# A dense trunk kernel: inside a chunk of weights the rounded-format products come first, then each f16 correction together

## The chip, the cores and the metric

The kernel runs on one core of one Trainium2 chip. Its time is the device time of one execution in microseconds; three executions took 3231.93, 3232.30 and 3233.21 us, median 3232.3 us. The trace comes from one more, profiled execution of the same program.

Five engines work side by side and are joined by semaphores: PE (TensorE, matrix products; its weight loads are listed as PEld), ACT (ScalarE), DVE (VectorE), POOL (GpSimd) and SP (SyncE, which here only issues DMAs). Each takes its own instructions in the order in which they stand in its queue.

## The reference

512 tokens of width 1024 pass through two layers. Everything is float32. Cut to what matters here:

```python
for layer in range(2):
    proj = h @ w_in[layer]                       # 1024 -> 11 776 columns, split into 14 parts
    y_a = (silu(rg) * rms_norm(retention(rq, rk, rv))) @ ret_w_out[layer]
    y_b = (silu(hg) * rms_norm(hgrn2_scan(hq, log_f, h_k, h_v)) * g) @ hgrn_w_out[layer]
    y_c = swa_with_sinks(sq, sk, sv) @ swa_w_out[layer]
    merged = sigmoid(ga) * y_a + sigmoid(gb) * y_b + sigmoid(gc) * y_c
    h = layer_norm(ALPHA * h + merged @ w_o[layer])
    ff = swiglu(h) if layer == 0 else moe_swiglu(h)   # dense 2816, then top 2 of 8 experts of 3584
    h = layer_norm(ALPHA * h + ff)
```

The dense products are all the `@` of this loop but the experts: `w_in`, the three branch projections, `w_o`, and the first layer's feed-forward block.

## The kernel before

**Three products for one.** A float32 product is made of three that PE takes at a higher pace. A weight chunk arrives as float32 (`raw`) and is split in three: `whi`, the value rounded to PE's fp32r format; `wlo`, what the rounding left, as f16; and a third part, the value itself as f16, which stands in the second half of the tile `wlo`. The activations are split alike: `hThi` (fp32r), `hTlo` (f16 rest) and `hT` (f16 value; `br...`, `fin...` and `hid...` are the same three for other activations). A dense product is then whi*hThi + (rest of w)*(f16 x) + (f16 w)*(rest of x), summed in one PSUM bank. I call the first the rounded product and the other two the corrections. Three such matmuls for one slice of 128 input rows are a triple.

**How the work is tiled.** Input rows come in 8 slices k of 128 (22 for the second product of the feed-forward block). A chunk of weights is 128x1024 numbers: in `proj_f` it is one block of 128 output columns over all 8 slices, the weights stand in the array and 512 tokens stream past (8 triples). In `proj_t` the activations stand in the array (128 tokens j out of 4) and 512 output columns stream; there a chunk holds 2 slices of k, and four PSUM banks, one for each j, fill together. `proj_t` holds the last four chunks of a product at once and goes through them j by j, 8 triples for one j; the 22 slices of the feed-forward block begin with seven chunks that are taken one at a time (4 j x 2 slices, 8 triples each). `proj_f_halves` works like `proj_f` on 256 tokens at a time. So nearly all dense work comes in groups of 8 triples.

**What sets the order.** PE's order is the order of the code (a hand-made schedule; small tasks of the mixers are slipped in by `soon`, `tick` and `need`). ACT, DVE and POOL are ordered by the framework's scheduler, so that their order may move when PE's does. `Stream` prepares weights: DMA into `raw` (L209), ACT writes `whi` (L226), DVE `wlo` (L227), ACT the f16 value (L234); there are five sets of `whi`/`wlo`, and `proj_t` holds four of them. After a layer norm the activations are turned by PE (L307), and `split` writes their three parts: ACT L355 (`hThi`), ACT L356 (`hT`), DVE L357 (`hTlo`); `need(j)` puts those turns of token block j into PE's queue. Every matmul of the program is recorded at L302. The experts of the second layer have code of their own (`accumulate`, `by_row`), with all rounded products of a chunk ahead of its corrections; `gu` is their PSUM tile.

Of the kernel before, what the change touches and what calls it, by code (L numbers as in the profile page):

```python
# [21 lines left out]
P = 128  # L22
D = 1024
S = 512
NJ = S // P
KD = D // P
# [164 lines left out]
class Stream:  # L191
# [58 lines left out]
    def done(self):  # L250
        self.held = 0
        self.fill()
# [5 lines left out]
def body(tc, A, out, dbg=None):  # L258
# [50 lines left out]
    T = PE  # L309
# [12 lines left out]
    def tick(budget=4.0):  # L322
        end = PE.clock + budget
        while PE.clock < end:
            due = [t for t in later if t[0] <= PE.clock]
            if not due:
                return

            task = max(due, key=lambda t: getattr(t[1], "prio", 0))
            later.remove(task)  # L330
            task[1](*task[2])
# [24 lines left out]
        SC.activation(x16, src, AF.Copy, scale=1.0 / (DS * LS))  # L356
        V.scalar_tensor_tensor(lo, hi.bitcast(F32), -DS * LS, src, op0=OP.mult, op1=OP.add)  # L357

    def mm3(ps, w, x, first, last):
        T.matmul(ps, w[0], x[0], start=first, stop=False)  # L360
        T.matmul(ps, w[1], x[2], start=False, stop=False)
        T.matmul(ps, w[2], x[1], start=False, stop=last)

    hbuf = []
    turns = {}
# [42 lines left out]
    def need(*js):  # L408

        for j in js:  # L410
            if j in turns:
                turns.pop(j)()
# [7 lines left out]
    def new_hT():  # L420
        hi = hpool.tile([P, KD, S], FR, name="hThi")
        lo = hpool.tile([P, KD, S], F16, name="hTlo")
        x16 = hpool.tile([P, KD, S], F16, name="hT16")
        return hi, lo, x16
# [6 lines left out]
    def proj_f(hT, kn=KD):  # L431
        need(*range(NJ))
        w = stream.next()
        ps = psA.tile([P, S], F32, name="acc")
        for k in range(kn):
            sl = slice(k * P, (k + 1) * P)
            mm3(ps, [t[:, sl] for t in w], [t[:, k] for t in hT], k == 0, k == kn - 1)
        tick()
        return ps


    def proj_f_halves(hT, n):
        ws = stream.take(n)
        pss = []
        for i in range(n):
            ps = psA.tile([P, S], F32, name="acc")
            pss.append(ps)
        need(0, 1)
        for th in range(2):
            tk = slice(256 * th, 256 * th + 256)  # L450
            for i, (ps, w) in enumerate(zip(pss, ws)):
                if th == 0 and i >= n - 2:
                    need(i - n + 4)
                for k in range(KD):
                    sl = slice(k * P, (k + 1) * P)
                    mm3(ps[:, tk], [t[:, sl] for t in w], [t[:, k, tk] for t in hT], k == 0, k == KD - 1)
        stream.done()
        return pss


    def proj_t(xT, kn, per, n, done=None):
        pss = []
        for j in range(NJ):
            ps = psA.tile([P, n], F32, name="acc")
            pss.append(ps)

        def tile_(j, k, w, q):
            tj = slice(j * P, (j + 1) * P)
            sl = slice(q * n, (q + 1) * n)
            T.matmul(pss[j], xT[0][:, k, tj], w[0][:, sl], start=(k == 0), stop=False)  # L470
            T.matmul(pss[j], xT[2][:, k, tj], w[1][:, sl], start=False, stop=False)
            T.matmul(pss[j], xT[1][:, k, tj], w[2][:, sl], start=False, stop=(k == kn - 1))

        nch = kn // per
        last = min(4, nch)
        for c in range(nch - last):
            need(*range(NJ))
            w = stream.next()
            for j in range(NJ):
                for q in range(per):  # L480
                    tile_(j, c * per + q, w, q)
            tick()
        ws = stream.take(last)
        for j in range(NJ):
            need(j)
            for i, w in enumerate(ws):
                if i == last - 1:
                    need(j + 1)
                for q in range(per):
                    tile_(j, (nch - last + i) * per + q, w, q)  # L490
            if j == NJ - 1:
                stream.done()
            if done is not None:
                done(j, pss[j])
            tick()
        return pss

    def out_ln(pool, xT, kn, per, g_ap, b_ap, nxt, after=None):
        gb = pool.tile([P, D], F32, name="ln_g", bufs=1)
        SC.dma_start(gb, rows(g_ap))  # L500
        bb = pool.tile([P, D], F32, name="ln_b", bufs=1)
        SC.dma_start(bb, rows(b_ap))
        V.tensor_scalar(bb, bb, LS, None, op0=OP.mult)
        old = hbuf[0]
        rs = []
        for j in range(NJ):
            r = pool.tile([P, D], F32, name="ln_r", bufs=4)
            SC.dma_start(r, old[j * P:(j + 1) * P])
            rs.append(r)
        new_hbuf(nxt)  # L510
        hT = new_hT()

        def done(j, ps):
            sl = slice(512 * half, 512 * half + 512)
            V.scalar_tensor_tensor(rs[j][:, sl], rs[j][:, sl], ALPHA / LS, ps, op0=OP.mult, op1=OP.add)
            ln_stats(pool, j, rs[j], half)
            if half:
                ln_tile(pool, j, rs[j], gb, bb, hT, None, after, spread=LN_SPREAD[j])
                if j >= 2:
                    need(j - 2)  # L520

        for half in range(2):
            proj_t(xT, kn, per, 512, done)
        return hT
# [10 lines left out]
    hT = new_hT()  # L535
# [29 lines left out]
    for i in range(2):  # L565
        t = const.tile([P, NJ, P], F32, name=f"adiag{i}")
# [64 lines left out]
    def token_major(tok, name, hT, func, pss=None):  # L631
        t = tok.tile([P, NJ, 512], F32, name=name)
        for j, ps in enumerate(pss or proj_t(hT, KD, 2, 512)):
            SC.activation(t[:, j], ps, func)
        return t

    def ret_qk(pool, hT, rot):
        qk = []
        for which in range(2):
            ps = proj_f(hT)  # L640
            sw = pool.tile([P, S], F32, name="sw", bufs=2)
            SC.activation(sw[0:64], ps[64:128], AF.Copy)
            SC.activation(sw[64:128], ps[0:64], AF.Copy)
            t = pool.tile([P, S], F32, name="rqk", bufs=4)
            V.tensor_tensor(t, ps, rot[:, 0], OP.mult)
            G.tensor_tensor(sw, sw, rot[:, 1], OP.mult)
            G.tensor_tensor(t, t, sw, OP.add)
            qk.append(t)
        return qk
# [28 lines left out]
    def hgrn_in(pool, layer, h, hT, lbs, first):  # L678
        ps = first.pop(0) if first else proj_f(hT)
        f = pool.tile([P, S], F32, name="hf", bufs=3)  # L680
        k = pool.tile([P, S], F32, name="hk", bufs=2)
        SC.activation(f, ps, AF.Sigmoid)
        SC.activation(k, ps, AF.Sigmoid, scale=-1.0)
        if layer > 0:
            V.tensor_scalar(f, f, lbs[:, 4, h:h + 1], lbs[:, 3, h:h + 1], op0=OP.mult, op1=OP.add)
            V.tensor_scalar(k, k, lbs[:, 4, h:h + 1], None, op0=OP.mult)
        ps = first.pop(0) if first else proj_f(hT)
        q = pool.tile([P, S], F32, name="hq", bufs=3)
        SC.activation(q, ps, AF.Copy)
        return f, k, q  # L690
# [300 lines left out]
    def dense_ffn(hT, g_ap, b_ap):  # L991
        first = proj_f_halves(hT, 4)
        settle()
        e_ffn, e_ln = ExitStack(), ExitStack()
        pool = e_ffn.enter_context(tc.tile_pool(name="ffn", bufs=1, reuse_waits="tile"))
        hi = pool.tile([P, KF, S], FR, name="hidhi")
        lo = pool.tile([P, KF, S], F16, name="hidlo")
        x16 = pool.tile([P, KF, S], F16, name="hid16")
        with tc.tile_pool(name="act", bufs=1, reuse_waits="tile") as lp:
            for f in range(KF):  # L1000
                pg = first.pop(0) if first else proj_f(hT)
                t = lp.tile([P, S], F32, name="fg", bufs=2)
                SC.activation(t, pg, AF.Silu)
                pu = first.pop(0) if first else proj_f(hT)
                V.scalar_tensor_tensor(t, pu, LS, t, op0=OP.mult, op1=OP.mult)
                split(t, hi[:, f], lo[:, f], x16[:, f])
        lp = e_ln.enter_context(tc.tile_pool(name="lnp", bufs=1, reuse_waits="tile"))
        hT = out_ln(lp, (hi, lo, x16), KF, 2, g_ap, b_ap, "f")
        norm_pools.extend([e_ln, e_ffn])
        return hT  # L1010
# [624 lines left out]
    hT = mixers(0, hT, A["ln_mix_g"][0], A["ln_mix_b"][0])  # L1635
    if stages >= 2:
        hT = dense_ffn(hT, A["ln_ffn_g"][0], A["ln_ffn_b"][0])
    if stages >= 3:
        hT = mixers(1, hT, A["ln_mix_g"][1], A["ln_mix_b"][1], route if stages >= 4 else None)
# [45 lines left out]
```

## Time and profile before

| | us |
|---|---|
| median of three executions | 3232.3 |
| the profiled execution | 3230.3 |
| span from first to last instruction in it | 3228.5 |
| PE busy | 3074.4 (95%) |
| DVE busy | 1968.9 (61%) |
| ACT busy | 2013.1 (62%) |
| POOL busy | 774.7 (24%) |

The dense work fills the first two thirds (to about 2150 us), the experts the rest. A matmul's recorded end is modelled and overlaps the next one, so a pace is read from the starts of like instructions, and not from the durations.

### The profile page before, as it was taken

How to read it: one execution, taken by the hardware profiler on the slowest of the kernel's cores; microseconds unless marked ns; L12 is line 12 of the kernel's file. 1: busy time of each engine (PE TensorE's matmuls, PEld its weight loads, DVE VectorE, ACT ScalarE, POOL GpSimd, SP SyncE). 2: the span in 40 equal slices, each digit the busy share in tenths (PEclk: the TensorE clock that was granted, in tenths of full speed). 3: DMA queues.
4: the chain of work that ended last, by engine and by line, in shares of the span. 5: the costliest groups of instructions: out<-in, count | busy, mean ns of one | idle time of the engine just before them, and what ended most of it. 6: DMA issues, size and time to landing. Idle time of an engine off the chain costs nothing. (4 is left out here: it accounts for less than half of the span.)

```text
span 3228.5 us, 51045 instructions
## 1 busy us (share of the span) xinstructions
PE 3074.4 (95%) x20186; PEld 2028.8 (63%) x20186; DVE 1968.9 (61%) x2393; ACT 2013.1 (62%) x2921; POOL 774.7 (24%) x541
## 2 busy tenths in 40 slices
PE   6999899999999999999899999969999999999996
PEld 3545454544454444545554554459999999999794
DVE  4666723333533334657743333469888898989998
ACT  5775545545555535784544555448778787888785
POOL 1234500111200001125410111214233242232442
PEclk9999999999999999999899999969999999999998
DMA  4111222222422243112222222349999999999995
GB/s 161 60 57 58 79 94 93 87 85 92 146 99 98 98 137 110 65 52 66 72 86 79 92 94 94 118 181 347 331 327 347 330 348 344 360 342 377 387 376 203
DMA packets 108466, 562.63 MB, mean 174 GB/s; under 512 B 13114, under 2 KB 13162, under 8 KB 75964
## 3 DMA queue, kind: packets, MB, share of 16 engines
q1 hardware_dynamic: 96768, 522.23, 45.3%
q10 hardware_dynamic: 6732, 24.34, 2.0%
q0 software_dynamic: 4720, 12.72, 1.2%
q8 instruction: 161, 2.64, 0.3%
q14 instruction: 85, 0.70, 0.1%
HBM read 545.39 MB, written 13.85 MB: 173 GB/s over the span
## 5 line engine op out<-in xcount | busy, mean ns | idle before, releaser
L227 DVE SCALAR_TENSOR_TENSOR wlo<-raw,whi 128x1024 f16<-128x1024 f32 (+2 forms) x662 | 1178.0, 1783 | 561.9 <-ACT whi L226 559.8
L226 ACT ACTIVATE whi<-raw 128x1024 fp32r<-128x1024 f32 (+2 forms) x662 | 973.5, 1472 | 601.2 <-PE acc L302 471.8
L302 PEld LDWEIGHTS <-wlo 128*128 128x128 f16 x8320 | 481.5, 98 | 441.0 <-issue 413.2
L302 PE MATMUL acc<-hThi,whi 128*128 128x512 f32 (+1 forms) x1312 | 747.9, 570 | 4.6 <-ACT hThi L355 4.6
L302 PE MATMUL acc<-hT,wlo 128*128 128x512 f16 (+1 forms) x1312 | 507.6, 387 | 0.1
L302 PE MATMUL gu<-xg,whi 128*128 128x288 f32 (+6 forms) x3584 | 496.2, 291 | 5.8 <-DVE gt L1444 2.7
L302 PE MATMUL acc<-hTlo,wlo 128*128 128x512 f16 (+1 forms) x1312 | 493.0, 376 | 1.9 <-DVE hTlo L357 1.9
L302 PEld LDWEIGHTS gu<-xg,whi 128*128 128x128 f32 x3584 | 454.2, 190 | 7.8 <-ACT whi L226 3.4
L1448 POOL TENSOR_TENSOR gs<-gs,gt 128x288 f32<-128x288 f32 (+6 forms) x112 | 255.4, 2280 | 584.6 <-ACT gs L1447 584.2
L302 PEld LDWEIGHTS acc<-hThi,whi 128*128 128x128 f32 x1312 | 251.7, 192 | 155.7 <-issue 8.8
L302 PE MATMUL acc<-whi,hThi 128*128 128x512 f32 (+1 forms) x576 | 320.9, 558 | 13.6 <-ACT hThi L355 12.8
L234 ACT ACTIVATE wlo<-raw 128x1024 f16<-128x1024 f32 x314 | 329.2, 1049 | 6.4 <-POOL ln_r L388 3.2
L302 PE MATMUL gu<-xh,wlo 128*128 128x144 f16 (+6 forms) x3584 | 245.0, 222 | 1.8 <-DVE wlo L227 1.4
L302 PE MATMUL acc<-wlo,hT 128*128 128x512 f16 (+1 forms) x576 | 220.9, 384 | 2.2 <-DVE wlo L227 2.1
L302 PE MATMUL acc<-brhi,whi 128*128 128x512 f32 x384 | 222.9, 581 | 0.0
L302 PE MATMUL acc<-wlo,hTlo 128*128 128x512 f16 (+1 forms) x576 | 214.5, 372 | 0.3 <-DVE hTlo L357 0.3
L302 PE MATMUL gu<-hd,whi 128*128 128x288 f32 (+4 forms) x1344 | 194.7, 296 | 0.0
L302 PEld LDWEIGHTS gu<-hd,whi 128*128 128x128 f32 x1344 | 175.6, 189 | 0.3
L302 PEld LDWEIGHTS acc<-whi,hThi 128*128 128x128 f32 x576 | 111.3, 193 | 77.7 <-ACT hThi L355 14.1
L302 PE MATMUL acc<-br,wlo 128*128 128x512 f16 x384 | 149.8, 390 | 0.0
L388 POOL TENSOR_TENSOR ln_r<-ln_r,ln_b 128x512 f32<-128x512 f32 x26 | 39.7, 1547 | 450.6 <-DVE ln_r L387 442.2
L302 PE MATMUL acc<-brlo,wlo 128*128 128x512 f16 x384 | 145.5, 379 | 0.0
(291 smaller groups left out, 3960.4 us busy)
## 6 DMA issues: line engine op xcount, KB each, us to landing
raw<-in_w_gu SPq DMA_DIRECT2D x224, 1024.0 KB, 7.0
raw<-in_w_l SPq DMA_DIRECT2D x248, 512.0 KB, 3.5
raw<-in_w_dn SPq DMA_DIRECT2D x96, 896.0 KB, 5.2
raw<-in_w_ffn SPq DMA_DIRECT2D x66, 512.0 KB, 3.4
raw<-in_w_dr SPq DMA_DIRECT2D x28, 1024.0 KB, 6.7
hspillm<-ln_r ACTq DMA_DIRECT2D x8, 512.0 KB, 2.6
ybuf<-ys ACTq DMA_DIRECT2D x5, 512.0 KB, 9.7
ln_r<-in_x SPq DMA_DIRECT2D x4, 512.0 KB, 10.5
```

Source lines behind the costliest of these rows:

```text
L226: nc.scalar.activation(hi[:, :n], raw, AF.Copy, scale=scale)
L227: nc.vector.scalar_tensor_tensor(lo[:, :n], raw, scale, hi[:, :n].bitcast(F32), op0=OP.mult, op1=OP.subtract)
L234: nc.scalar.activation(lo[:, 1024:1024 + n], raw, AF.Copy, scale=1.0 / LS)
L302: nc.tensor.matmul(out_, lhsT, rhs, start=start, stop=stop)
L388: G.tensor_tensor(r[:, sl], r[:, sl], bb[:, sl], OP.add)
L1448: G.tensor_tensor(s, s, t[:, 1], OP.mult)
```

## The change

Within a group the matmuls change places: `mm3` now takes all slices, and issues the rounded product of every slice, then the first correction of every slice, then the second. In `proj_t` the chunks that are taken one at a time get all rounded products (for every j), then for each j both corrections; the last four chunks get, for each j, the rounded products of all four, then the first corrections of all four, then the second. `need(j + 1)` moves from in front of the last chunk to in front of the last correction. Nothing is added or left out.

```diff
-    def mm3(ps, w, x, first, last):
-        T.matmul(ps, w[0], x[0], start=first, stop=False)
-        T.matmul(ps, w[1], x[2], start=False, stop=False)
-        T.matmul(ps, w[2], x[1], start=False, stop=last)
+    def mm3(ps, w, x, kn, tk=slice(None)):
+
+        for wi, xi in ((0, 0), (1, 2), (2, 1)):
+            for k in range(kn):
+                T.matmul(ps, w[wi][:, k * P:(k + 1) * P], x[xi][:, k, tk], start=(wi + k == 0),
+                         stop=(wi == 2 and k == kn - 1))
...
-        for k in range(kn):
-            sl = slice(k * P, (k + 1) * P)
-            mm3(ps, [t[:, sl] for t in w], [t[:, k] for t in hT], k == 0, k == kn - 1)
+        mm3(ps, w, hT, kn)
...
-        def tile_(j, k, w, q):
+        def tile_(part, j, k, w, q):
...
-            for j in range(NJ):
-                for q in range(per):
-                    tile_(j, c * per + q, w, q)
+            for parts in ((0,), (1, 2)):
+                for j in range(NJ):
+                    for part in parts:
+                        for q in range(per):
+                            tile_(part, j, c * per + q, w, q)
...
-            for i, w in enumerate(ws):
-                if i == last - 1:
+            for part in range(3):
+                if part == 2:
                     need(j + 1)
-                for q in range(per):
-                    tile_(j, (nch - last + i) * per + q, w, q)
+                for i, w in enumerate(ws):
+                    for q in range(per):
+                        tile_(part, j, (nch - last + i) * per + q, w, q)
```

PE's queue at the start of the program, the first token block of the first `proj_t`, stood before as follows (names are output<-moving,stationary, with tile numbers; `whi_105`, `whi_114`, `whi_123` and `whi_130` are the four chunks; a rounded product loads its weights itself, an f16 one has a LDWEIGHTS of its own):

```order
L307 MATMUL mx_224<-ident_75,ln_r_94 128x128 x4
L302 MATMUL acc_205<-whi_105,hThi_87 128x512
L302 LDWEIGHTS hT16_89
L302 MATMUL acc_205<-wlo_106,hT16_89 128x512
L302 LDWEIGHTS hTlo_88
L302 MATMUL acc_205<-wlo_106,hTlo_88 128x512
...
L302 MATMUL acc_205<-whi_114,hThi_87 128x512
...
L307 MATMUL mx_250<-ident_75,ln_r_101 128x128 x4
L307 MATMUL mx_258<-ident_75,ln_r_101 128x128 x4
L302 MATMUL acc_205<-whi_130,hThi_87 128x512
```

And now:

```order
L307 MATMUL mx_224<-ident_75,ln_r_94 128x128 x4
L302 MATMUL acc_205<-whi_105,hThi_87 128x512 x2
L302 MATMUL acc_205<-whi_114,hThi_87 128x512 x2
L302 MATMUL acc_205<-whi_123,hThi_87 128x512 x2
L302 MATMUL acc_205<-whi_130,hThi_87 128x512 x2
L302 LDWEIGHTS hT16_89
L302 MATMUL acc_205<-wlo_106,hT16_89 128x512
...
L302 MATMUL acc_205<-wlo_131,hT16_89 128x512
L307 MATMUL mx_248<-ident_75,ln_r_101 128x128 x4
L307 MATMUL mx_256<-ident_75,ln_r_101 128x128 x4
L302 LDWEIGHTS hTlo_88
L302 MATMUL acc_205<-wlo_106,hTlo_88 128x512
```

The rounded products of all four chunks and all eight slices now stand ahead of the first correction, and the turns of the next token block stand behind 16 of the 24 products instead of 18.

ACT's queue where the first half of the output projection goes over into the second (the names with numbers are the weight chunks of the second half and the one behind it), before:

```order
L226 ACTIVATE whi_6308<-raw_6306 128x1024
L234 ACTIVATE wlo_6309<-raw_6306 128x1024
L226 ACTIVATE whi_6315<-raw_6313 128x1024
L234 ACTIVATE wlo_6316<-raw_6313 128x1024
L226 ACTIVATE whi_6329<-raw_6327 128x1024
L234 ACTIVATE wlo_6330<-raw_6327 128x1024
```

And now:

```order
L226 ACTIVATE whi_6308<-raw_6306 128x1024
L226 ACTIVATE whi_6315<-raw_6313 128x1024
L226 ACTIVATE whi_6329<-raw_6327 128x1024
L234 ACTIVATE wlo_6309<-raw_6306 128x1024
L234 ACTIVATE wlo_6316<-raw_6313 128x1024
L234 ACTIVATE wlo_6330<-raw_6327 128x1024
```

The scheduler has put the three `whi` first. SP's queue is the same in both kernels.

## Rows read from the trace of the kernel before

**Rows 1.** The page: busy tenths of PE in 40 slices of the span.
```profile
PE   6999899999999999999899999969999999999996
```

**Rows 2.** Busy time by stretch: all engines, then clock, DMA share and GB/s.
```profile
400.00:600.00 200.00, 200.00 (x955) 102.71 (x954) 65.57 (x91) 98.40 (x154) 17.19 (x19) 1.00 0.26 86
1250.00:1264.00 14.00, 10.97 (x37) 4.58 (x35) 10.78 (x14) 8.99 (x13) 1.20 (x1) 0.76 0.60 206
```

**Rows 3.** Groups by line and shape, PE: out<-moving,stationary, count, busy us, mean ns.
```profile
L302 PE MATMUL acc<-hThi,whi 128*128 128x512 f32 x1248 | 723.7, 580 | 0.0
...
L302 PE MATMUL acc<-whi,hThi 128*128 128x512 f32 x512 | 298.1, 582 | 13.6 <-ACT hThi L355 12.8 <-ACT whi L226 0.8
L302 PE MATMUL acc<-brhi,whi 128*128 128x512 f32 x384 | 222.9, 581 | 0.0
...
L302 PE MATMUL acc<-whi,hidhi 128*128 128x512 f32 x176 | 102.2, 580 | 0.0
L302 PE MATMUL acc<-whi,finhi 128*128 128x512 f32 x128 | 76.0, 594 | 0.0
```

**Rows 4.** Timeline at 300 us, PE and its weight loads: start, duration.
```profile
299.79 0.58 PE L302 MATMUL acc<-whi,hThi 128*128 128x512 f32 x1
...
300.44 0.19 PEld L302 LDWEIGHTS acc<-whi,hThi 128*128 128x128 f32 x1
...
300.89 0.39 PE L302 MATMUL acc<-wlo,hT 128*128 128x512 f16 x1
...
301.12 0.38 PE L302 MATMUL acc<-wlo,hTlo 128*128 128x512 f16 x1
...
302.50 0.58 PE L302 MATMUL acc<-whi,hThi 128*128 128x512 f32 x1
```

**Rows 5.** Timeline of PE in the last expert's second product.
```profile
3167.85 1.02 PE L302 MATMUL gu<-wlo,hh 128*112 128x512 f16 x4
3168.52 2.22 PE L302 MATMUL gu<-whi,hd 128*112 128x512 f32 x8
...
3176.01 1.02 PE L302 MATMUL gu<-wlo,hh 128*112 128x512 f16 x4
```

**Rows 6.** Timeline of PE in an expert's first product.
```profile
2606.91 1.12 PE L302 MATMUL gu<-xh,wlo 128*128 128x136 f16 x16
...
2609.91 1.12 PE L302 MATMUL gu<-xh,wlo 128*128 128x136 f16 x16
```

**Rows 7.** Timeline at the start of the program, PE.
```profile
25.96 0.63 PE L302 MATMUL acc<-wlo,hTlo 128*128 128x512 f16 x1
...
37.18 0.79 PE L302 MATMUL acc<-whi,hThi 128*128 128x512 f32 x1 [10.59 <-ACT hThi L355]
```

**Rows 8.** Timeline at the start of the second layer, ACT and PE.
```profile
1257.64 1.06 ACT L226 ACTIVATE whi<-raw 128x1024 fp32r<-128x1024 f32 x1 [0.97 <-DVE ln_r L391]
...
1258.75 0.80 PE L302 MATMUL acc<-whi,hThi 128*128 128x512 f32 x1 [0.82 <-ACT whi L226]
...
1261.25 0.65 PE L302 MATMUL acc<-wlo,hT 128*128 128x512 f16 x1
...
1261.69 0.63 PE L302 MATMUL acc<-wlo,hTlo 128*128 128x512 f16 x1
```

**Rows 9.** Timeline at the start of the feed-forward block, PE.
```profile
883.23 0.38 PE L302 MATMUL acc<-hThi,whi 128*128 128x256 f32 x1 [4.60 <-ACT hThi L355]
...
885.85 0.37 PE L302 MATMUL acc<-hTlo,wlo 128*128 128x256 f16 x1 [1.86 <-DVE hTlo L357]
```

**Rows 10.** Waits of PE: waited for, us in total, times, longest us.
```profile
PE mx L302 <- ACT adiag L750: 14.6, 4, 6.5
PE mx L302 <- DVE adiag L742: 9.2, 2, 5.0
...
PE mx L302 <- DVE ql L732: 7.8, 2, 4.0
...
PE acc L302 <- ACT whi L226: 0.8, 1, 0.8
```

More of the change, by code (lines that the diff above doesn't have):

```diff
@@ L453, in proj_f_halves @@
                     need(i - n + 4)
-                for k in range(KD):
-                    sl = slice(k * P, (k + 1) * P)
-                    mm3(ps[:, tk], [t[:, sl] for t in w], [t[:, k, tk] for t in hT], k == 0, k == KD - 1)
+                mm3(ps[:, tk], w, hT, KD, tk)
         stream.done()
@@ L465, in proj_t @@
             pss.append(ps)
-        def tile_(j, k, w, q):
+        def tile_(part, j, k, w, q):
             tj = slice(j * P, (j + 1) * P)
             sl = slice(q * n, (q + 1) * n)
-            T.matmul(pss[j], xT[0][:, k, tj], w[0][:, sl], start=(k == 0), stop=False)
-            T.matmul(pss[j], xT[2][:, k, tj], w[1][:, sl], start=False, stop=False)
-            T.matmul(pss[j], xT[1][:, k, tj], w[2][:, sl], start=False, stop=(k == kn - 1))
+            wi, xi = ((0, 0), (1, 2), (2, 1))[part]
+            T.matmul(pss[j], xT[xi][:, k, tj], w[wi][:, sl], start=(part + k == 0), stop=(part == 2 and k == kn - 1))
         nch = kn // per
```

## The prediction

> **What bounds the kernel now.** I read the page's slices first. The reader is to see that PE is busy nearly all the time, in the dense two thirds (slices 2 to 27) as in the experts [rows 1]. The busy time by stretch then shows that nothing stands behind it there: in 400 to 600 us PE is busy for all of 200 us, ACT for 98, DVE for 66, and the DMA engines for a quarter [rows 2]. So a dense group is worth what PE needs for it, and the question is what PE loses inside a triple.
>
> The groups by shape count the triples: 1248 + 512 + 384 + 176 + 128 = 2448 rounded products of 512 columns, each with two corrections [rows 3]. That is 306 groups of 8. (128 triples of half the width, 64 in `proj_f_halves` and 64 in the SWA values, are left out: by the ratio below they are worth 1 us.)
>
> The timeline gives the pace. Rounded products start at 299.79 and, four triples later, at 302.50: 0.678 us a triple, 5.42 us a group [rows 4]. The second correction starts 0.23 us behind the first. Where f16 products stand in a row, the step is shorter: four of them cover 1.02 us and one lasts 0.38 [rows 4, 5], so three steps take 0.64, or 0.213 each. A triple of such steps would be 0.64, so 0.04 us of each triple is lost around the rounded product.
>
> **What the change moves, and what each part is worth.** Nothing is removed; the count of matmuls and weight loads stays. What goes is the alternation: a group has 8 passages from rounded to f16 and 8 back, and will have one of each.
>
> *The pace of the new order.* The trace of before already holds it, in the last expert's second product: 8 rounded products in a row, then 4 f16, all of 512 columns. Its f16 quartets start at 3167.85 and, three blocks later, at 3176.01: 2.72 us a block with both passages in it [rows 5]. Less four f16 steps (0.86, at 0.215) that leaves 1.86 us for 8 rounded products and the two passages, 0.232 each. A new dense group is that block and 12 more f16 steps: 2.72 + 2.58 = 5.30 us. Against 5.42 it saves 0.12 us, and 306 groups save 36.7 us. The weights that stand there have 112 columns and those here 128; that is the weak place of the step. Bounds: nothing, if the 0.04 belongs to every rounded product of 128 columns whatever its neighbours; and 40 us by the experts' first product, which does have 128 columns: 16 rounded products of 272 streamed columns and 16 f16 of 136 take 3.00 us [rows 6]. At 0.215 us for 512 columns those 6528 would take 2.74; the 0.26 over is 0.016 for each rounded product, passages included, so a group would take 24 x 0.215 + 8 x 0.016 = 5.29 us, and 306 groups save 40. I take 36.7, by the row with the same 512 columns.
>
> [...] The weight load of a rounded product takes 0.19 us and starts at 300.44, which is where the f16 product before it starts too (301.12 less 0.68) [rows 4]; and 8 rounded products in a row, with their loads, take 1.86 us [rows 5]; so the load lies beside the product before it, a rounded one too. [...]
>
> *Who is needed earlier.* A token block of `proj_t` now wants the `whi` of all four chunks within its first 6 rounded products (6 x 0.23 = 1.4 us), where it had 6 triples (4.1 us); the f16 parts are wanted later. In the trace of before PE waited for `whi` once among the dense products, 0.8 us [rows 10]: it is mostly ready long ahead. Three places are not:
>
> - Start of the program. PE sits idle for 10.59 us until the second half of the first token block's `hThi` comes at 37.18. Before that it had done four whole triples, the last of them from 25.96 [rows 7]. Now it can do four rounded products, and 8 corrections fall behind the wait: 8 x 0.215 = +1.7 us.
> - Start of the second layer. The fourth chunk's `whi` is made from 1257.64 and PE goes on at 1258.75 [rows 8], with two triples to do. Now 2 rounded and all 16 corrections stand behind it: 12 matmuls more, 2.6 us at full pace. [...]
> - Start of the feed-forward block. PE got its first rounded and first f16 product at 883.23, and then waited 1.86 us for `hTlo` [rows 9]. That is now wanted last, and the rounded and f16-value products fill the wait: -2 us.
>
> Together +2.2 us. Where the first half of `w_o` gives way to the second, `whi` comes late too, but ACT's new order makes three of them first, so I add nothing there.
>
> *What is given back.* In the HGRN stage PE waits for chains that run over DVE and ACT: 14.6 + 9.2 + 7.8 = 31.6 us in 8 waits [rows 10]. These chains do not become shorter, so what PE saves between their start and the wait goes into the wait. A chain spans up to some four groups of 0.12 us, so 8 x 4 x 0.12 = 3.8 us at most there, and nothing at least; with the short waits of the attention stage I take +3 us.
>
> The sum: -36.7 - 1 + 2.2 + 3 = -32.5 us. The profiled execution took 3230.3 us, which makes 3197.8. The median of the runs is 2.0 us above it, so I predict 3200 us.
>
> **Rivals.**
>
> *A. More is given back.* ACT and DVE have been ordered anew by the scheduler (some hundred places), and the dense stages of the mixers lean on them. If half of the gain of the mixers (some 230 of the 306 groups, 28 us) goes into waits, the time is 3200 + 14 = 3214. For it: the 8 waits above and many of under 1 us. Against it: ACT and DVE are under half busy in most of the stretch [rows 2].
>
> *B. The gain is larger.* The pace term is the 40 us of its upper bound, nothing is given back, and the layers' starts cost nothing, because the new order of ACT's queue helps there as at `w_o`: 3232.3 - 41 = 3191. For it: the weights of [rows 6] have 128 columns. Against it: at the two starts PE waits for one certain part, and what was done ahead of it is now behind it.
>
> *C. No change.* The lost 0.04 us belongs to the rounded product and not to the passage; then only the places above count, 3232.3 + 2.2 = 3235. Against it stands the block of [rows 5], with 0.232 for a rounded product and its share of the passages, where before a triple less two steps leaves 0.678 - 0.43 = 0.248. [...]
>
> *D. Slower: `whi` comes late at every entry.* The place is the first token block of each `proj_t`, 24 entries in all (11 a layer and 2 in the feed-forward block). Where ACT's queue holds the fourth `whi` behind an eviction, PE waits, as at the second layer's start, with 16 corrections still to do. One such entry costs up to 3 us; from 11 late entries on it eats the gain, and with all 24 the time is 3200 + 72 = 3272. Against it: 0.8 us of waits for `whi` today, and the scheduler's new order of `whi`.
>
> *E. Slower: the weight loads come into the open.* A rounded product's load does not go on beside another rounded product, and 7 in each group pay 0.19 us: 3232 + 407 = 3639. [...] Against it stands the 0.232 us step of [rows 5].
>
> **Numbers.** Forecast 3200 us, chance 0.63, its own range 3193 to 3208. A 0.15, B 0.10, C 0.07, D 0.04, E 0.01. A measurement of this kernel tells about 0.2% (6.5 us) from no change, so faster is the forecast with A and B, 0.88; same is C, 0.07; slower D and E, 0.05. The range 3187 to 3221 takes in the forecast, A and B with some room on both sides, about 0.85, and leaves C, D and E out.
>
> **What would show it.** Right: rounded products in a row step by 0.23 us and f16 by 0.215, and a group takes 5.30 us where it took 5.42; PE's busy time falls by about 35 us before 2150 us, and the experts start some 32 us earlier and last as long. PE's wait at the start of the feed-forward block is gone, and the first `proj_t` of each layer ends 2 us later behind its wait. Wrong: rounded products step by 0.245 or more (C), or by 0.40 (E); the waits of PE grow by more than 6 us (A); waits for `whi` of over 10 us (D).

## The result, and the profile after

| | before | after |
|---|---|---|
| median, us (range, runs) | 3232.1 (3230.8 to 3233.6, 6) | 3215.8 (3214.5 to 3219.2, 6) |
| ratio to before, 95% interval | | 0.9950 (0.9938 to 0.9963) |
| the profiled execution, us | 3230.3 | 3219.2 |
| span, us | 3228.5 | 3217.5 |
| PE busy, us | 3074.4 | 3040.2 |
| span less PE busy, us | 154.1 | 177.3 |

The change gains 16.4 us by the medians, half of the 32 forecast, inside the range; rival A's 3214 was nearer than the forecast. The profiled execution of after lies 3.5 us above the median of its runs, so between the two profiles the gain is 11.1 us, and that is the amount which the traces have to explain. The last three rows of the table already tell how: PE needs 34.2 us less for the same matmuls, and stands still for 23.2 us more.

The pace came as forecast. The timeline of PE after, in the feed-forward block's second product (start, duration, count):

```profile
1122.32 2.19 PE L302 MATMUL acc<-whi,hidhi 128*128 128x512 f32 x8
1124.35 0.61 PE L302 MATMUL acc<-wlo,hid 128*128 128x512 f16 x2
...
1127.62 2.19 PE L302 MATMUL acc<-whi,hidhi 128*128 128x512 f32 x8
...
1132.93 1.27 PE L302 MATMUL acc<-whi,hidhi 128*128 128x512 f32 x4
```

Start to start a group takes 5.30 and 5.31 us, where four triples took 2.71 [rows 4]. Between starts inside a row, a rounded product takes 0.231 us and an f16 one 0.216. Plain float32 products, which the HGRN stage has, were slower in before at the same clock of 1.00: four of 128 columns (`hqd` with `hkd`, 8 records) took 0.98 us, from 303.37 to 304.35, where a triple of 512 columns takes 0.68 in before and 0.66 now.

What came back as idle time is in PE's list of waits after (waited for, us in total, times, longest us):

```profile
PE acc L302 <- ACT hThi L355: 22.3, 3, 14.5
PE mx L302 <- ACT adiag L750: 16.6, 4, 6.7
...
PE mx L302 <- DVE adiag L742: 10.3, 2, 5.7
...
PE mx L302 <- DVE ql L732: 8.6, 2, 4.4
...
PE acc L302 <- ACT whi L226: 6.9, 2, 4.4
PE mx L307 <- ACT spt L863: 6.6, 7, 1.6
PE mx L302 <- DVE ssb L838: 6.5, 6, 2.4
...
PE acc L302 <- ACT finhi L355: 4.1, 2, 2.1
...
PE mx L302 <- ACT spt L863: 2.5, 4, 1.1
PE mx L307 <- DVE ssb L838: 1.9, 2, 0.9
PE acc L302 <- ACT brhi L355: 1.0, 2, 0.5
```

The three HGRN rows (`adiag` twice, `ql`) sum to 35.5 us, 3.9 more than the 31.6 of [rows 10]. The four of the attention stage (`spt`, `ssb`) sum to 17.5; the same four of before make 12.5 (4.0, 3.2, 2.7 and 2.6). `whi` was 0.8 and is 6.9. Two rows are new: `finhi` and `brhi`.

An idle time is not yet a loss, since work may have moved to its other side. So I cut both traces at the same products and compared the stretches (the boundary is the product's start in before; the forecast is its own terms, dealt out by groups; it sums to -32.3 by rounding):

| stretch, to the start of | us in before | forecast | measured |
|---|---|---|---|
| the SWA values, layer 1 | 71.4 | +1.0 | +2.0 |
| retention (SWA, HGRN between) | 398.0 | -3.0 | +2.6 |
| `w_o`, first half | 833.0 | -8.6 | -7.4 |
| `w_o`, second half | 854.8 | -0.5 | **+3.6** |
| layer 2 | 1250.4 | -10.4 | -9.5 |
| the SWA values, layer 2 | 1291.1 | +1.8 | +2.0 |
| retention | 1620.5 | -3.0 | +0.2 |
| `w_o`, first half | 2055.4 | -8.6 | -7.4 |
| `w_o`, second half | 2077.2 | -0.5 | **+3.6** |
| end | 3228.5 | -0.5 | -0.7 |

Two things stand out: `w_o`, 8.1 us off in two stretches of 22 us, and SWA with HGRN, 8.8 us off.

**The start of `w_o`.** PE and ACT of before (a product's start; ACT's product of `finhi`):

```profile
833.00 0.58 PE L302 MATMUL acc<-whi,finhi 128*128 128x512 f32 x1
...
837.76 0.58 PE L302 MATMUL acc<-whi,finhi 128*128 128x512 f32 x1
```
```profile
836.42 0.63 ACT L355 ACTIVATE finhi<-sg 128x512 fp32r<-128x512 f32 x1 [2.42 <-POOL sg L915]
```

And of after, PE, then ACT:

```profile
830.18 1.98 PE L302 MATMUL acc<-whi,finhi 128*128 128x512 f32 x7
834.23 0.69 PE L302 MATMUL acc<-whi,finhi 128*128 128x512 f32 x1 [2.07 <-ACT finhi L355]
834.73 3.42 PE L302 MATMUL acc<-wlo,fin 128*128 128x512 f16 x8
837.98 1.89 PE L302 MATMUL acc<-wlo,finlo 128*128 128x512 f16 x8
...
855.52 0.81 PE L302 MATMUL acc<-whi,finhi 128*128 128x512 f32 x2
```
```profile
833.55 0.63 ACT L355 ACTIVATE finhi<-sg 128x512 fp32r<-128x512 f32 x1 [3.21 <-POOL sg L915]
```

The last of the eight slices of the activations is finished only 4.0 us after PE begins the product (4.05 in before): the last merge runs over DVE, POOL and ACT. In before the eighth rounded product stood behind 7 triples, 4.76 us in, and `finhi` was there 0.71 us ahead of it (836.42 + 0.63 = 837.05). Now it stands 1.6 us in. PE waits 2.07 us, and then does 8 f16 products in 3.42 us where the next 8 take 1.89. The busy time by stretch says why (the last three numbers: clock, DMA share, GB/s):

```profile
833.00:838.00 5.00, 3.77 (x10) 1.40 (x11) 0.85 (x2) 2.21 (x3) 0.52 (x1) 0.66 0.67 195
```

The granted clock is 0.66 of full in these 5 us, and 0.50 from 834.6 to 837.8, where the f16 products come 0.43 us apart instead of 0.216; in before the window from 833 to 838 had 1.00. The half of `w_o` took 21.76 us and takes 25.34 (830.18 to 855.52), and in layer 2 as long: 2.07 us of waiting, and by the starts of the rows 0.3 more for the eighth rounded product and 1.5 more for the 8 f16 ones.

**SWA.** The dearest new wait stands once in each layer. DVE of after, then POOL, then PE:

```profile
149.80 2.92 DVE L227 SCALAR_TENSOR_TENSOR wlo<-raw,whi 128x1024 f16<-128x1024 f32 x1
...
152.93 0.68 DVE L838 TENSOR_TENSOR ssb<-mx,wmask 128x512 f32<-128x512 f32 x1
```
```profile
149.74 1.91 POOL L852 TENSOR_TENSOR ssb<-ssb,sst 128x1024 f32<-128x1024 f32 x1 [6.40 <-PE mx L307]
```
```profile
153.66 0.38 PE L302 MATMUL mx<-skh,sqt 128*128 128x256 f32 x1 [2.38 <-DVE ssb L838]
```

POOL, then DVE of before:

```profile
146.91 1.89 POOL L852 TENSOR_TENSOR ssb<-ssb,sst 128x1024 f32<-128x1024 f32 x1 [5.65 <-DVE sst L851]
```
```profile
148.06 0.75 DVE L843 SCALAR_TENSOR_TENSOR sst<-sst,sinks 128x4 f32<-128x4 f32 x1
148.74 1.21 DVE L227 SCALAR_TENSOR_TENSOR wlo<-raw,whi 128x1024 f16<-128x1024 f32 x1
...
150.34 1.29 DVE L838 TENSOR_TENSOR ssb<-mx,wmask 128x512 f32<-128x512 f32 x2
```

A weight split stands ahead of the `ssb` for which PE waits, in both kernels. In before it starts as POOL's instruction ends (146.91 + 1.89 = 148.80), and takes 1.21 us. In after POOL's starts 0.06 us ahead of it, and the split takes 2.92: it ends 1.07 behind POOL. At 1.21 it would have ended at 151.0, and the wait of 2.38 would be shorter by 1.7. In before the small instruction ahead of it met POOL instead: L843 took 0.75 us, where others like it take 0.15, and ended with POOL's. DVE's order has changed there too: in before two longer instructions (L842 and L886) stand between the reciprocal whose result POOL takes (L851) and the split, in after only three short ones (L843 to L845). So the moment at which the split meets POOL, and DVE's order that sets this moment, are not told apart here.

### The profile page after: what moved, and what is told of

The parts are those of the page before. It is cut to its first block, busy times and chain, and to the rows that moved or that the text cites. A ratio compares the mean times of both kernels' runs of the same rounds, so it can differ in the third digit from the quotient of the medians.

```text
span 3217.5 us, 51030 instructions
## 1 busy us (share of the span) xinstructions
PE 3040.2 (94%) x20186; PEld 2193.9 (68%) x20186; DVE 1969.7 (61%) x2393; ACT 2026.3 (63%) x2921; POOL 767.5 (24%) x541
## 5 line engine op out<-in xcount | busy, mean ns | idle before, releaser
L302 PEld LDWEIGHTS <-wlo 128*128 128x128 f16 x8320 | 600.9, 98 | 417.8 <-issue 53.6
L302 PE MATMUL acc<-hThi,whi 128*128 128x512 f32 (+1 forms) x1312 | 351.2, 410 | 5.6 <-ACT hThi L355 5.6
L302 PE MATMUL acc<-hT,wlo 128*128 128x512 f16 (+1 forms) x1312 | 307.1, 377 | 0.0
L302 PE MATMUL acc<-hTlo,wlo 128*128 128x512 f16 (+1 forms) x1312 | 303.5, 374 | 0.0
L302 PE MATMUL acc<-whi,hThi 128*128 128x512 f32 (+1 forms) x576 | 150.6, 403 | 23.6 <-ACT hThi L355 16.7
L703 POOL TENSOR_TENSOR he<-he,hf 128x256 f32<-128x256 f32 x112 | 98.9, 885 | 150.9 <-DVE hf L711 74.7
L302 PE MATMUL acc<-wlo,hT 128*128 128x512 f16 (+1 forms) x576 | 132.9, 375 | 0.0
L302 PE MATMUL acc<-wlo,hTlo 128*128 128x512 f16 (+1 forms) x576 | 129.2, 367 | 0.0
L1443 ACT ACTIVATE gt<-gu 128x288 f32<-128x288 f32 (+6 forms) x224 | 85.4, 381 | 55.5 <-PE gu L302 54.6
L852 POOL TENSOR_TENSOR ssb<-ssb,sst 128x1024 f32<-128x1024 f32 (+1 forms) x32 | 55.5, 1734 | 266.3 <-DVE sst L843 153.5
```

The lines of the kernel that those rows point to most:

```text
L302: nc.tensor.matmul(out_, lhsT, rhs, start=start, stop=stop)
L703: G.tensor_tensor(ev[:, :, 0], ev[:, :, 0], cv[:, :, 1, hw - 1:hw].broadcast_to([P, nb, hw]), OP.mult)
L852: G.tensor_tensor(s[:, :, w0:], s[:, :, w0:], st[:, 3, :, None].broadcast_to([P, GQ, nw]), OP.mult)
L1443: SC.activation(t, ps[:, :, cap:2 * cap], AF.Copy)
```

## The experiments

Two theories stood after this. Theory 1: the loss is at a few places where the first token block of a product (or its first chunk) now wants all eight slices at once, and in SWA and HGRN, whose chains take back any pace. The rival: these waits are paid anyway, the real limit lies elsewhere, and mending them moves the idle time on. In the kernels below a set is the number of slices that go through the three passes together: 8 in after, 1 is the old triple.

| kernel | median, us (range) | ratio to before (95%) |
|---|---|---|
| after | 3215.8 (3214.5 to 3219.2) | 0.9950 (0.9938 to 0.9963) |
| E1 triples at the start of `w_o` | 3211.5 (3210.9 to 3214.7) | 0.9935 (0.9922 to 0.9949) |
| E2 E1 and at the other starts | 3208.5 (3208.0 to 3210.6) | 0.9927 (0.9913 to 0.9940) |
| E3 triples in SWA and HGRN alone | 3215.3 (3212.9 to 3217.8) | 0.9948 (0.9934 to 0.9961) |
| E4 sets of 4 | 3219.0 (3214.3 to 3220.2) | 0.9953 (0.9940 to 0.9967) |
| E5 sets of 2 | 3230.1 (3228.4 to 3233.7) | 0.9993 (0.9984 to 1.0002) |
| E6 E2 and E3 | 3206.1 (3205.0 to 3206.5) | 0.9915 (0.9902 to 0.9929) |
| E7 E2, triples in SWA | 3206.0 (3205.2 to 3208.6) | 0.9918 (0.9904 to 0.9931) |
| E8 E2, triples in HGRN | 3205.3 (3203.6 to 3207.6) | 0.9914 (0.9900 to 0.9927) |

Before took 3232.8 beside E1 to E4, and 3233.0 beside E5 to E8. The intervals of neighbouring kernels overlap, so a difference of a few us between two of them is read here beside their traces, not alone.

**E1.** In the first half of `w_o`, the first token block goes in triples (`SET`, the number of slices in a set, is 8 here):

```diff
-            proj_t(xT, kn, per, 512, done)
+            proj_t(xT, kn, per, 512, done, (lambda j: 1 if j == 0 else SET) if half == 0 and kn == KD else None)
...
+            m = sets(j) if sets else SET
+            for u0 in range(0, len(units), m):
...
+                    for i, q in units[u0:u0 + m]:
+                        tile_(part, j, (nch - last + i) * per + q, ws[i], q)
```

> The changed kernel, but the first token block (j = 0) of the first half of the output projection w_o goes in triples again, in both layers; all else in the new order. Theory 1 (operands that come late): the new pace is there in full (5.306 us a group against 5.427, 36.6 us in all) and is given back where the first rounded products of a product want an operand that is still being made; the dearest place is the start of w_o, where the last slice of the merged activations comes 4.05 us after the first product and is wanted after 1.6. There PE idles 2.07 us and then runs at the lower clock; each layer loses 4 us against a start in triples. Expected: no idle time before the eighth slice, the first half of w_o 21.3 us instead of 25.3, the total 8 us below the changed kernel, ratio to before about 0.9925. Rival (the missing time went into the chains of the attention and HGRN stages or into the new order of ACT and DVE): at most 1 us better than the changed kernel, ratio 0.995.

It gains 4.3 us by the medians and 7.8 between the profiled executions. The timeline of PE in E1 shows the place itself (its line numbers are one higher):

```profile
829.41 0.58 PE L303 MATMUL acc<-whi,finhi 128*128 128x512 f32 x1
...
834.17 0.58 PE L303 MATMUL acc<-whi,finhi 128*128 128x512 f32 x1
...
850.84 1.51 PE L303 MATMUL acc<-whi,finhi 128*128 128x512 f32 x5
```

No wait, and 21.43 us for the half (829.41 to 850.84) where after took 25.34: 3.9 us in each layer, as theory 1 said. The mechanism is shown; its price by the medians, 4.3, is smaller than the expected 8. The trace of E3, further down, has the same wait without the low clock, and there the half takes 23.64: 2.2 us above E1's in each layer, 4.4 in both. After's profiled execution is the slowest of its six and has the lowest mean granted clock (0.977, the others 0.979 to 0.980). So the low clock probably follows the wait in some executions of after and not in others; that is inferred, since only one execution of a kernel has a trace.

**E2.** E1, and triples in the first token block of each layer's first `proj_t`, and in the first product of each merge:

```diff
-        pss = proj_t(hT, KD, 2, 512)
+        pss = proj_t(hT, KD, 2, 512, None, lambda j: 1 if j == 0 else SET)
...
-            ps = proj_f(br)
+            ps = proj_f(br, n=1 if d == 0 else None)
```

> As the one before, and the first token block of the first product of each layer (HGI) and the first branch product of each gated merge (d = 0) go in triples too. Theory 1: the start of the program gives back 2.3 us, that of the second layer 2.7, the two third merges 1.1 each, the two starts of w_o 4 each: 15 us in all, so about 3201 us, ratio 0.9905. Rival (the chains of the attention and HGRN stages hold the missing time): the starts are worth less than 4 us together, ratio 0.994 or more.

3 us below E1 and 7 below after, where 15 were expected in all: less than theory 1 said, more than the rival's 4. Compared with after in the same stretches, the start of the program gave 2.2 us back and that of layer 2 1.9, but SWA and HGRN then took 3.9 us more than in before where after's took 2.6 more (layer 2: 1.1 and 0.2). The waits for `adiag`, `ql` and `ssb` are as long as in after, so they do not show where these 1.3 and 0.9 us went, and it stays open. In these first token blocks the triples also put `need(j + 1)` back in its old place; the run does not tell the two apart.

**E3.** Only the dense products inside SWA and HGRN go in triples (`n=1` in `proj_f`, `lambda j: 1` in `proj_t`):

```diff
-                ps = proj_f(hT)
+                ps = proj_f(hT, n=1)
...
-        for j, ps in enumerate(proj_t(hT, KD, 4, 256)):
+        for j, ps in enumerate(proj_t(hT, KD, 4, 256, None, lambda j: 1)):
...
-        g = token_major(tok, "tokg", hT, AF.Silu)
+        g = token_major(tok, "tokg", hT, AF.Silu, None, lambda j: 1)
```

> The changed kernel, but every dense product of the sliding-window attention and of the HGRN stage (some 42 groups a layer) goes in triples again. The changed kernel's profile has this stretch at 339.9 us in the first layer and 340.2 in the second, where before it took 337.5 and 340.2, although 42 groups are worth 5 us of pace. Theory 1: chains over ACT and DVE set the time of this stretch, so it is as long in triples: total within 3 us of the changed kernel, ratio 0.994 to 0.996. Theory 2 (the new order costs this stretch more than the chains, by late operands and ACT and DVE ordered anew): the stretch falls to 337.5 in the first layer, total 2 to 3 us below the changed kernel. Rival (pace bounds this stretch and the time went elsewhere): 10 us above the changed kernel, ratio 0.998.

The same median as after, though 38 groups in each layer are slower by 0.12 us each, 4.6 us a layer: the pace is worth nothing there. In E3's trace the stretch that the expectation names even takes 337.6 us in layer 1 and 338.7 in layer 2, 2.3 and 1.5 less than in after, which is what theory 2 had named. So the chains take back the whole pace, and the new order costs a little on top of it. (E3's profiled execution is its fastest and after's its slowest, so the sign is surer than the size.)

The trace of E3 shows one thing more. `w_o` is in the new order here and waits as in after, but the clock stays up (PE, then the busy time by stretch, with clock, DMA share and GB/s last):

```profile
832.29 0.50 PE L303 MATMUL acc<-whi,finhi 128*128 128x512 f32 x1 [2.06 <-ACT finhi L356]
832.63 1.90 PE L303 MATMUL acc<-wlo,fin 128*128 128x512 f16 x8
```
```profile
831.00:836.00 5.00, 3.71 (x18) 1.78 (x18) 0.89 (x2) 2.21 (x3) 0.57 (x1) 1.00 0.57 186
```

The 8 f16 products behind the wait take 1.90 us instead of 3.42, and the half 23.64 instead of 25.34, in both layers.

**E4 and E5.** Sets of 4 and of 2 (`SET = 4`, `SET = 2`), in all groups but the 14 of the feed-forward block's chunks that are taken one at a time, which keep the order of after:

```diff
+SET = 4
...
-            for k in range(kn):
+        for k0 in range(0, kn, n):
+            for wi, xi in ((0, 0), (1, 2), (2, 1)):
+                for k in range(k0, min(kn, k0 + n)):
```

> The changed kernel with sets of 4 slices instead of 8: four rounded products, four first corrections, four second ones, and again. Each group then has 2 passages each way instead of 1 (before: 8). If the lost time is one price for each pair of passages, (5.427 - 5.306) / 7 = 0.017 us, a group takes 5.323 us and 306 groups lose 5.3 us of pace. By theory 1 the late operands cost less: at w_o the last slice is wanted 3.6 us after the start instead of 1.6, at the start of the program 12 products stand ahead of the wait again, at that of the second layer 12 instead of 6: some 9 us back. Total 3 to 5 us below the changed kernel, ratio 0.9935 to 0.994. Rival (late operands are not the cause): only the pace changes, 5 us above the changed kernel, ratio 0.9965.

> Every group of 8 slices goes in sets of two: two rounded products, then their first corrections, then their second. A group has then 4 passages from rounded to f16 and back, where the changed kernel has 1, the sets of four had 2 (5.340 us a group in the feed-forward block) and the kernel before 8 (5.427). Theory 1 (the price of a passage falls with their number, 0.033 for the second and 0.0145 for each behind it): 5.369 us a group. Rival (each passage costs the same, 0.0173): 5.358. Rival (it is the row of three f16 products or more that is fast, and two rounded ones in a row gain nothing): 5.40 or more. As a time: 306 groups at +0.06 against the changed kernel make +19 us less what the waits of w_o, the starts, SWA and HGRN give back (8 to 15), so 3220 to 3227, ratio about 0.997.

E4 was expected 3 to 5 us below after and came out no better (3 us above it by the medians, with overlapping ranges); E5 was expected at 3220 to 3227 and came at 3230. The timelines of PE in the feed-forward block, first E4, then E5:

```profile
1001.92 1.28 PE L303 MATMUL acc<-hThi,whi 128*128 128x512 f32 x4
...
1007.26 1.28 PE L303 MATMUL acc<-hThi,whi 128*128 128x512 f32 x4
```
```profile
1003.94 0.82 PE L303 MATMUL acc<-hThi,whi 128*128 128x512 f32 x2
...
1009.32 0.81 PE L303 MATMUL acc<-hThi,whi 128*128 128x512 f32 x2
```

A group of 8 takes 5.34 us in sets of 4 (two sets, 1001.92 to 1007.26) and 5.38 in sets of 2 (four sets, 1003.94 to 1009.32). The median group of the block's first product takes 5.307 in one set, 5.340 in two, 5.378 in four, and 5.427 in eight: the first extra passage costs 0.033 us, the next two 0.019 each, the last four 0.012 each. So sets of 4 cost twice the pace that I had counted on (0.033 instead of 0.017 a group), but that is not the whole of it. In the same stretches as above, E4 gets 6.7 us back against after at the two starts of `w_o` (that half takes 21.98 us) and 2.7 at the layers' starts; it loses 3.5 in retention, the merges and the feed-forward block, 5.3 in SWA and HGRN, where pace counts for nothing, and 1.6 in the last stretch. In E5 the pace is still 0.05 us a group better than before, some 15 us in all, and the time is that of before within 0.2%. Against before it loses 4.4 us in SWA and HGRN of layer 1 and 4.1 in layer 2, and E4 loses 5.3 and 2.8: the new order of the products costs there even where little is gained from it.

**E6, E7, E8.** E2 with triples in both SWA and HGRN, in SWA alone, in HGRN alone (the lines of E3, all or some of them).

> The changed kernel with the old order of triples at the three places where the new one waits (first half of w_o, first token blocks of the HGRN input product of each layer, first product of each gated merge) and in all dense products of the SWA and HGRN stages. So the new order is left in the retention stage, the merges behind their first product, the second half of w_o and the feed-forward block. Theory 1 (SWA and HGRN are held by chains over ACT and DVE, so their pace is worth nothing, and the three places cost what the runs so far showed): the gains add up, 2 to 5 us below the kernel with the three places alone (3208.5), so 3204 to 3206, ratio about 0.9915. Rival (what the saved waits give is taken back by the next chain, whatever the order there): 3208 to 3211, ratio 0.993. Rival (pace counts in SWA and HGRN as elsewhere): 5 to 10 us above 3208.5, ratio 0.995.

> As the kernel with the three places in triples, and the SWA stage's dense products in triples too (HGRN's in the new order). It tells in which of the two stages the pace is taken back. If the chains of SWA hold (the waits before skh that DVE ssb ends): 3205 to 3208, and PE reaches the HGRN stage no later than in the kernel with the three places alone. If only the HGRN chains hold: some 2 to 4 us above it, 3211 to 3213, since some 10 groups a layer lose 0.12 us each.

> As the kernel with the three places in triples, and the HGRN stage's dense products in triples too (SWA's in the new order). If the HGRN chains hold (adiag, ql): 3204 to 3208, with the start of the retention stage no later than in the kernel with the three places alone, in both layers. If only the SWA chains hold: 4 to 6 us above it, 3212 to 3215, some 20 groups a layer at 0.12 us.

All three are 2 to 3 us below E2 and cannot be told apart from each other. They are 10 us below after and 27 to 28 below before: the best versions here, with the old order where PE is fed by others, and the new one in retention, the merges, the second half of `w_o` and the feed-forward block. The waits show which stage does what. E7 (SWA in triples), then E8 (line numbers 12 higher than in after: `ssb` L838 is L850 here):

```profile
PE mx L303 <- ACT adiag L762: 15.5, 4, 6.7
PE mx L303 <- DVE adiag L754: 10.9, 2, 6.2
PE mx L303 <- DVE ql L744: 8.6, 2, 4.4
...
PE mx L303 <- DVE ssb L850: 3.2, 6, 0.6
```
```profile
PE mx L303 <- ACT adiag L762: 14.4, 4, 6.3
PE mx L303 <- DVE adiag L754: 9.3, 2, 5.0
PE mx L303 <- DVE ql L744: 7.8, 2, 4.0
PE mx L303 <- DVE ssb L850: 6.5, 6, 2.4
```

In E7 the long `ssb` wait is gone (2.4 to 0.6) and the HGRN chain costs 35.0; in E8 the `ssb` wait stands and the HGRN chain is at 31.5, that of before. That each of the two gives as much as both is not explained by this. What the triples do for SWA they may do by the order of DVE or by the moment at which POOL meets it; I did not try these apart, and it stays open.

## Why the prediction came out half right

**The pace: right.** 5.30 us a group was forecast, 5.30 to 5.31 measured; PE's busy time fell by 34.2 us for some 35. The row that carried it, 8 rounded products in a row in the experts [rows 5], held for weights of 128 columns too. With it fell C (steps of 0.231, not 0.245) and E: in after's trace the eight weight loads of such a row run beside its products.

```profile
1122.29 1.79 PEld L302 LDWEIGHTS acc<-whi,hidhi 128*128 128x128 f32 x8
```

The eight loads, 0.19 us each, lie within 1.79 us, and the products start 0.231 apart, where E had them at 0.40. The 0.215 of the sum stands in no row (they give 0.213); in after's trace the f16 steps are 0.216, so it was near enough.

**The starts: the mechanism right where it is shown here, one size off.** The program's start lost 2.0 us where +1.0 was forecast net of pace, the second layer's 2.0 for 1.8. In the +2.2 of the sum the second layer's start counts 2.5, which was my estimate and which no run shows by itself: the runs have a clock of 0.50 of full there in both orders (before from 1256 to 1262 us, with f16 steps of 0.44 [rows 8]; after from 1248 to 1254, with its first 8 corrections in 3.26 us), and the loss of 2.0 is 2.7 without the 0.7 of pace that the forecast of this stretch took off the 2.5. At the program's start I had priced the corrections behind the wait at full pace, 0.215 us each; there they came 0.43 us apart (eight starts from 39.34 to 42.35). Layer 2 shows the mechanism as told, in two waits: PE has four, then two, then two rounded products, and all corrections behind them.

```profile
1245.35 0.73 PE L302 MATMUL acc<-whi,hThi 128*128 128x512 f32 x2 [2.53 <-ACT whi L226]
1250.44 1.22 PE L302 MATMUL acc<-whi,hThi 128*128 128x512 f32 x2 [4.36 <-ACT whi L226]
1251.46 3.26 PE L302 MATMUL acc<-wlo,hT 128*128 128x512 f16 x8
```

The wait for `hTlo` at the feed-forward block is gone too: the corrections run on without a stop. But the wait ahead of the block grew from the 4.60 us of [rows 9] to 5.60, and the stretch from the second half of `w_o` to there took 0.5 us longer than before, where pace alone would have made it 0.5 shorter.

```profile
884.54 2.20 PE L302 MATMUL acc<-hThi,whi 128*128 128x256 f32 x8 [5.60 <-ACT hThi L355]
886.54 1.93 PE L302 MATMUL acc<-hT,wlo 128*128 128x256 f16 x8
888.26 1.40 PE L302 MATMUL acc<-hTlo,wlo 128*128 128x256 f16 x8
```

**The step that failed first: "so I add nothing there", of `w_o`.** I asked only which weights are needed earlier, and only where the first half gives way to the second. At the first half's own start it is the activations that are needed earlier: all eight slices of `finhi` within 1.6 us instead of 4.8, and the last had 0.7 us to spare. That slack stands in the trace of before, in the rows shown under "The start of `w_o`", and one subtraction would have shown the wait: 837.05 less (833.00 + 1.6) is 2.4 us. With the low clock behind it, it cost 4.1 us in each layer against the forecast, 8.1 of the 21 that are missing between the profiles; with the clock up, as in E3's trace, it costs 2.4. E1 takes it away and shows it. The starts of the merges are the same in small (`brhi`, 1.0 us of waits; 1.2 us off in each of the two stretches that hold them).

**The step that was too small: "I take +3 us" for what is given back.** The bound for the HGRN chain, 3.8, is what came, 3.9. The attention stage I had only waved at, and it gave back 5.0, of which 2 x 1.8 is the one wait behind the weight split. In all SWA and HGRN gave back the 9.0 that their 72 groups gain, and 2.8 more (+2.6 and +0.2 where -4.5 each stood without the +3): 11.8. Of it 8.9 shows as longer waits; the other 2.9 I could not assign. E3 and E6 to E8 show that this pace is worth nothing, and that the old order is a little better there; by what part of the new order (the products, or ACT and DVE ordered anew) stays open.

Of those 21.2 us, `w_o` and SWA with HGRN make 16.9, the merges' stretches 2.4; the rest is spread over the others. By the medians 16 are missing, and E6 to E8 bring 10 back (3205 to 3206 for the 3200 forecast), E6 without any of the pace of SWA and HGRN.

**Rival A** named the right mechanism, and its sign came (PE's waits grew by 23 us, where it asked for more than 6), but it was right for a part of the mixers only: SWA and HGRN gave back 8.8 us more than forecast, while the retention and the merges (72 of 122 groups in each layer) kept 14.8 of the 17.2 us forecast for their stretches. D's mechanism happened, not for `whi` at 24 entries but for `whi` at one and `finhi` at two.

## What to carry to other kernels

When products are regrouped so that one kind comes first, list for every group's start both operands, and take from the trace of before how long each slice was there ahead of its use; where that slack is shorter than the distance by which the use moves up, leave the old order at that one place. Count pace only for stretches in which the engine waits for nobody; where it waits for a chain over other engines, set what is saved to nothing, and the gain is what remains. And price a half measure (sets of 4) on the chip before trusting that its cost is linear.

## What was not expected of the hardware

- A short wait can cost more than itself, and need not. Behind 2.07 us without work at the start of `w_o`, PE's granted clock was 0.66 of full over 5 us in after, and 8 f16 products took 3.42 us instead of 1.89. In E3, behind 2.06 us at the same place, it stayed at 1.00. Behind the wait of 2.38 us in SWA, after had 0.58 over 4 us in layer 1 (154.5 to 158.5) and 1.00 in layer 2 (1365.5 to 1369.5).
- The price of going from f16 to rounded products and back fell with how often it was done: 0.033 us for the second passage in a group (E4), 0.019 each for the next two (E5), 0.012 each for the fifth to eighth (before).
- A DVE instruction stretched by nearly all of the time in which a POOL instruction ran beside it: the same split of 128x1024 weights took 1.21 us in before, and 2.92 in after, where POOL's 1.91 us had begun 0.06 ahead of it. A split that had begun first did not stretch: 1.22 us at 831.18 in after, where POOL's began 0.26 behind it. The long one ended 1.07 us behind POOL's, and PE waited 2.38 us for the `ssb` behind it; in before POOL's had begun 1.83 us ahead of the split, which took the 1.21.
